# A streaming encoder step: frame tiles of the first group loaded two steps later, kept weight sums stored by the sync queue, and another order of the opening

## The chip, the cores and the metric

The kernel runs on one core of a Trainium2 chip. A core has five engines with queues of their own: TensorE (PE, matrix products; PEld is its weight load), VectorE (DVE), ScalarE (ACT), GpSimd (POOL) and SyncE (SP, which here only issues transfers). Each engine works through its instructions in the order in which they stand, and semaphores make one wait for another. The metric is the device time of one execution in microseconds, lower is better; the time given is the median of several runs.

## The reference

One step of a streaming encoder layer (depth 1): 2048 frames of a new stream and 32 of a running one, 1024 channels, all in float32.

```
hn   = rmsnorm(h, g_mix)
proj = hn @ w_in                       # 1024 x 3072: hA, bA, cA, zA, vB, zB of 512 columns each
yA   = bA * causal_conv3(cA * hA) * silu(zA)
yB   = (pooled(vB) - vB, per-group linear map, scale) * silu(zB)     # windows 2, 4, 8, 16
h    = h + concat(yA, yB) @ w_out
gate = sigmoid(rmsnorm(h, g_ple) @ w_ple_gate)
h    = h + (p @ w_ple) * gate
y    = rmsnorm(h, g_final)             # and the last rows of cA*hA and vB as new states
```

## The kernel before, in words

**Numbers.** Every float32 operand of a large product is split into a high part, rounded to a type that TensorE multiplies in one pass, and a low part, the rest. `split` does it: ScalarE casts the high part, VectorE subtracts it from the source (lines 77 and 78). A product is three products: high by high, high by low, low by high.

**Groups.** The 2080 frames are five blocks of 416 (`NB`), taken in groups `[0, 1]`, `[2, 3]`, `[4]`. In each group the input projection runs over four units j of 128 columns. The very first unit computes its two blocks plainly (`Unit.plain`), block by block. The other units of the first two groups take the two blocks as a 2 by 2 scheme with seven products in place of eight (`Unit.seven`, `Unit.pair`): the frames go in as seven combinations (11, 21, T2, T1, T3, 22, T4), the weights of two kinds side by side (zb with v, c with h, za with b) as seven others. Sums of carried and fresh results are made by ScalarE (`carry`, line 866) and VectorE (`out`, line 869).

**The opening.** The gain row g_mix is spread over 128 partitions by two small products (`gm`, line 375), and VectorE copies them to `g_bc`. The frame tiles of block 0 (three of 128 rows, one with 32 rows each of blocks 0 and 1) are loaded, squared and summed on ScalarE (line 88), their rstd is made on GpSimd (lines 69 and 73), VectorE scales them by rstd and gain (line 406), TensorE turns them (line 413), and they are split into `B0`. Then the weights zb, v and c of the first unit are split. `project` runs the first product by high parts first (line 586), all others by `half_product` (line 571). The generator `second_block` puts block 1 and the combinations in between.

**Next group's frames.** While the first group computes, `next_columns` prepares the seven combinations for the second group, column by column (3, 0, 1, 2). Each step of `Unit.seven` calls `aside`, which advances it at a fixed pace. For a column `frame_sums` squares and scales two frame tiles, turns them, and writes seven split results into tiles of the pool `xin` (`staged`), each of which `to_memory` stores to memory through GpSimd's queue (line 482). `xin` has five slots and holds both the frame tiles `xt` and the staged results. `load_ahead` loads the next column's two frame tiles on the sync queue; it is called at the sixth of the column's steps (i == 5), behind the result "22" and ahead of "T2", "T3" and "T4".

**Kept sums.** `pair_weights` adds and subtracts the two kinds' raw weights (lines 547 and 535). In the first group the two results of a pair are stored to memory (`kept`, lines 552 and 553) and read again in the second group. The stores go through GpSimd's queue, which also carries the rstd steps and the stores of the staged results. The sync queue carries the loads of raw weights (line 508, a ring of four tiles `raws`), the loads of frame tiles (line 392) and the stores of y (line 712).

**What orders the work.** A tile framework places the instructions of each engine by its own reckoning and inserts the semaphores; `keep_in_program_order` pins single instructions. A tile in a ring waits until the previous user of its slot is through.

Of the kernel before, what the change touches and what calls it, by code (L numbers as in the profile page):

```python
# [9 lines left out]
F32 = mybir.dt.float32  # L10
# [5 lines left out]
P = 128  # L16
# [18 lines left out]
def trunk(ctx, tc, x_p, x_s, c_conv, c_pool, p_p, p_s, g_mix, w_in, conv_w, conv_b, pool_w,  # L35
# [294 lines left out]
    with ExitStack() as s1:  # L330
# [195 lines left out]
        def pair_weights(gi, ka, kb, j, name, ring, s_ring):  # L526
# [17 lines left out]
            else:  # L544
# [5 lines left out]
                if gi == 0:  # L550
                    kept[ka, j] = k1, k3 = [tc.dram_tile([P, KH, P], F32, name=f"kept_{name}_{q}") for q in (1, 3)]
                    nc.gpsimd.dma_start(k1, s_t)
                    nc.gpsimd.dma_start(k3, s3)
            src = {"11": a11, "12": a12, "S2": a11, "S1": s_t, "S3": s3, "S4": a12, "22": a22}
# [18 lines left out]

        begun = []

        def project(ps, w, tb):
            x = hn[tb]
            if begun:
                for half in range(2):
                    half_product(ps, w[half], x[half], half == 0, half == 1)  # L580
                return

            begun.append(tb)
            steps = sorted(((k, a, b) for k in range(KC) for a, b in ((0, 0), (0, 1), (1, 0))), key=lambda t: t[1:])
            for i, (k, a, b) in enumerate(steps):
                nc.tensor.matmul(ps[:, :NB], w[k // KH][:, k % KH, a], x[k // KH][:, k % KH, b], start=i == 0,
                                 stop=i == len(steps) - 1)


        B0 = {}  # L590
        ahead0 = [x_tile(f"0_{c}", [x_rows(0, c)]) for c in range(3)]
        short0 = x_tile("0_3", [x_rows(0, 3), x_rows(1, 3)])
# [76 lines left out]
        class Unit:  # L669
# [98 lines left out]
            def plain(self):  # L768
                tbs, j, tag, zs, V, U, c_s = self.tbs, self.j, self.tag, self.zs, self.V, self.U, self.c_s
                blocks = range(len(tbs))  # L770

                def product_of(kind, b, w):
                    ps = bank(f"{kind}{tag}_{tbs[b]}")
                    project(ps, w, tbs[b])
                    return ps[:, :NB]
# [730 lines left out]
```

## Time and profile before

| what | us |
|---|---|
| median of three runs | 945.69 (944.71 to 946.76) |
| the profiled execution | 946.5, of which the span of the core's work is 944.7 |
| TensorE busy | 922.9 |
| VectorE busy | 717.3 |
| ScalarE busy | 481.3 |
| GpSimd busy | 137.0 |
| transfers | 190.05 MB, mean 201 GB/s |

Times in the profile are counted from the start of the span. A row of the time order reads: start, length, engine, line, operation, result<-inputs, shape, how many, and in brackets how long the engine had stood idle before it and what released it. A row of a stretch reads: length, then busy time of TensorE, its weight loads, VectorE, ScalarE and GpSimd, the granted clock of TensorE, the busy share of the transfer engines, and GB/s. A row of waits reads: who waited for whom, us in total, times, longest. A row of transfers ends with the KB of each and the us from issue to landing; q0 is GpSimd's queue, with packets, MB and its share of the transfer engines.

### The profile page before, as it was taken

To read this page: it belongs to the slowest core of one execution; us is meant where nothing else is said; L and a number is where in the kernel's file an instruction comes from. 1 tells how busy PE (TensorE), PEld (TensorE's weight loads), DVE (VectorE), ACT (ScalarE), POOL (GpSimd) and SP (SyncE) were. 2 spreads that over 40 slices of the span, in tenths; PEclk is the share of its full clock that TensorE was granted. 3 is DMA by queue.
4 is the path that set the end of the run, shared out by engine and by line. 5 is a ranking of instruction groups with operands and counts; after the bars stand their busy time and mean duration, and the time that the engine had idled before them with its cause. 6 is when DMAs were issued, how large, how long until landed. Compare 5 with 4: busy or idle time off the path is not lost.

```text
span 944.7 us, 13128 instructions
## 1 busy us (share of the span) xinstructions
PE 922.9 (98%) x4599; PEld 832.6 (88%) x4599; DVE 717.3 (76%) x1212; ACT 481.3 (51%) x890; POOL 137.0 (14%) x262
## 2 busy tenths in 40 slices
PE   7999999898999999999999999999999999999996
PEld 5999999898999999999999987888878868888885
DVE  6797998788676877776777588766554798888995
ACT  5554555463344554443554356434434885556564
POOL 2202333230100120000000011211111000211113
PEclk9999999999999999999999999999999999999999
DMA  8347686686972554618655349875785884566562
GB/s 252 95 125 199 190 262 215 198 247 182 417 253 90 180 185 131 208 57 291 177 175 174 129 145 315 270 199 159 222 255 160 309 277 127 198 232 222 207 206 111
DMA packets 132639, 190.05 MB, mean 201 GB/s; under 512 B 11740, under 2 KB 101084, under 8 KB 131293
## 3 DMA queue, kind: packets, MB, share of 16 engines
q1 hardware_dynamic: 115149, 134.06, 45.4%
q0 software_dynamic: 14688, 49.65, 16.0%
q10 hardware_dynamic: 2736, 5.51, 1.8%
q8 instruction: 36, 0.59, 0.3%
q14 instruction: 30, 0.25, 0.1%
HBM read 129.59 MB, written 59.58 MB: 200 GB/s over the span
## 4 chain that ended last, share of the span: by engine, by line
PE 77%; DVE 2%; ACT 1%; issue 0%; POOL 0%; POOLq 0%; ACTq 0%
PE x_o L167 9%; PE x_g L167 9%; PE x_zab L571 5%; PE e L102 5%; PE z_g L167 5%; PE x_ch L571 5%; PE x_zbv L571 5%; PE z_o L167 4%; PE z_ch L571 3%; PE z_zbv L571 2%; PE z_zab L571 2%; PE y_g L167 2%; PE y_o L167 2%; PE b L571 2%; PE za L571 2%; PE c L571 2%
## 5 line engine op out<-in xcount | busy, mean ns | idle before, releaser
L77 ACT CAST y_S<-y_fS 128x512 fp32r<-128x512 f32 x32 | 19.5, 621 | 43.9 <-PE x_o L167 19.4
L102 PE MATMUL e<-wq,pps 128*128 128x512 f32 (+1 forms) x156 | 38.9, 399 | 0.2 <-ACT pps L77 0.2
L571 PE MATMUL z_ch<-B,w_ch_S 128*128 128x416 f32 x168 | 35.9, 364 | 3.3 <-ACT U L866 3.3
L406 DVE SCALAR_TENSOR_TENSOR xt<-xt,rstd_x,g_bc 128x1024 f32<-128x1024 f32 (+2 forms) x18 | 23.1, 1282 | 19.1 <-POOL rstd_x L73 17.7
L571 PE MATMUL x_zab<-B,w_zab_S 128*128 128x416 f32 x168 | 34.6, 353 | 2.7 <-ACT V L866 2.0
L571 PEld LDWEIGHTS z_ch<-B,w_ch_S 128*128 128x128 f32 x168 | 32.4, 195 | 4.1 <-ACT U L866 3.6
L167 PE MATMUL x_g<-wg_b,g_S 128*128 128x512 f32 x128 | 35.9, 390 | 0.0
L167 PE MATMUL x_o<-wo_b,y_S 128*128 128x512 f32 x128 | 35.8, 391 | 0.0
L571 PEld LDWEIGHTS x_zab<-B,w_zab_S 128*128 128x128 f32 x168 | 31.1, 188 | 4.0 <-ACT V L866 2.6
L571 PE MATMUL z_zab<-B,w_zab_S 128*128 128x416 f32 x168 | 34.1, 351 | 0.5 <-ACT U L866 0.5
L571 PE MATMUL z_zbv<-B,w_zbv_S 128*128 128x416 f32 x168 | 34.2, 352 | 0.0
L571 PE MATMUL x_zbv<-B,w_zbv_S 128*128 128x416 f32 x168 | 34.1, 351 | 0.0
L571 PE MATMUL x_ch<-B,w_ch_S 128*128 128x416 f32 x168 | 34.0, 351 | 0.0
L102 PEld LDWEIGHTS e<-wq,pps 128*128 128x128 f32 (+1 forms) x156 | 27.4, 182 | 6.9 <-ACT pps L77 0.5
L571 PEld LDWEIGHTS z_zab<-B,w_zab_S 128*128 128x128 f32 x168 | 31.3, 188 | 1.1 <-ACT U L866 0.8
L69 POOL TENSOR_SCALAR ms_f<-ssq_f 128x1 f32<-128x1 f32 (+1 forms) x15 | 8.8, 588 | 160.7 <-ACT junk L88 160.7
L571 PEld LDWEIGHTS x_ch<-B,w_ch_S 128*128 128x128 f32 x168 | 31.4, 188 | 0.3
L571 PEld LDWEIGHTS x_zbv<-B,w_zbv_S 128*128 128x128 f32 x168 | 31.3, 188 | 0.3
L571 PEld LDWEIGHTS z_zbv<-B,w_zbv_S 128*128 128x128 f32 x168 | 31.2, 188 | 0.4
L77 ACT CAST y<-y 128x512 fp32r<-128x512 f32 x24 | 14.8, 618 | 28.7 <-PE x_o L167 14.0
L1328 DVE SCALAR_TENSOR_TENSOR h<-h,rstd_f,g_bc 128x1024 f32<-128x1024 f32 (+1 forms) x15 | 19.3, 1284 | 12.7 <-POOL rstd_f L73 12.7
L167 PEld LDWEIGHTS x_o<-wo_b,y_S 128*128 128x128 f32 x128 | 24.0, 188 | 5.1 <-ACT c_o L1132 0.3
(582 smaller groups left out, 2670.8 us busy)
## 6 DMA issues: line engine op xcount, KB each, us to landing
y<-y_d SPq DMA_DIRECT2D x16, 512.0 KB, 7.7
x<-in_x_prompt_dram SPq DMA_DIRECT2D x16, 512.0 KB, 6.7
h_d<-x SPq DMA_DIRECT2D x16, 512.0 KB, 3.4
h<-h_d SPq DMA_DIRECT2D x16, 512.0 KB, 5.1
xt<-in_x_prompt_dram SPq DMA_DIRECT2D x15, 512.0 KB, 12.0
e<-e_d SPq DMA_DIRECT2D x15, 512.0 KB, 5.1
out_dram<-h POOLq DMA_DIRECT2D x14, 512.0 KB, 3.0
p_dT<-T POOLq DMA_DIRECT2D x12, 512.0 KB, 5.3
```

What stands on the lines that cost most here:

```text
L69: nc.gpsimd.tensor_scalar(ms[:n], ssq[:n], scalar1=1.0 / D, scalar2=EPS, op0=ALU.mult, op1=ALU.add)
L77: ins = nc.scalar.copy(hi, src)
L102: nc.tensor.matmul(ps[:n], pps[:, a, k, :n], wp[k][b][:, cs], start=k + q == 0, stop=k == 1 and q == 2)
L167: nc.tensor.matmul(ps[:n], lhs[:, k, a, :n], w[b][:, k], start=start and k + q == 0, stop=k == KH - 1 and q == 2, skip_group_check=True)
L406: nc.vector.scalar_tensor_tensor(xt[:n], xt[:n], r[:n], g_bc[:n], op0=ALU.mult, op1=ALU.mult)
L571: nc.tensor.matmul(ps[:, :NB], lhs[:, k, x], b[:, k, y], start=start and k + q == 0, stop=stop and k == KH - 1 and q == 2, skip_group_chec ...
L1328: nc.vector.scalar_tensor_tensor(h[:n], h[:n], rf[:n], g_bc[:n], op0=ALU.mult, op1=ALU.mult)
```

## The change

Three things change.

1. In `next_columns` the next column's frame tiles are loaded at i == 7 instead of i == 5: behind the last but one of the results.
2. The 18 stores of kept sums (nine pairs of kinds in the first group) go through the sync queue instead of GpSimd's.
3. The opening is written out. The two products of g_mix stay in their banks: VectorE scales the first frame tiles from there, in halves, and ScalarE copies them to `g_bc` later. TensorE gets 14 transposes of the identity whose results are not used, into the bank that the short tile takes later: seven behind the products of g_mix, and two, three and two behind the first three tiles' transposes. Casts and subtractions of the first block are put in a fixed order, one cast goes to VectorE, and the first halves of the zb weight are cast ahead of the short tile's. The first 72 products no longer run zb, then v, then c, but high by high for zb, v and c, then high by low for the three, then low by high (`first_products`).

```diff
@@ the opening
+        pg = [tbank(f"gm_{half}") for half in range(2)]
         for half in range(2):
-            cs = slice(half * NH, half * NH + NH)
-            pg = tbank(f"gm_{half}")
-            nc.tensor.matmul(pg, ones, gm_row[:, cs], start=True, stop=True)
-            nc.vector.tensor_copy(g_bc[:, cs], pg)
+            nc.tensor.matmul(pg[half], ones, gm_row[:, half * NH:half * NH + NH], start=True, stop=True)
+
+        def fill(n, t):
+            for _ in range(n):
+                tc.keep_in_program_order(nc.tensor.transpose(t[:, :P], ident, ident))
+
+        short_bank = bank("pt0_3")
+        fill(7, short_bank)
@@ pair_weights
-                    nc.gpsimd.dma_start(k1, s_t)
-                    nc.gpsimd.dma_start(k3, s3)
+                    nc.sync.dma_start(k1, s_t)
+                    nc.sync.dma_start(k3, s3)
@@ the first products
-        begun = []
-
         def project(ps, w, tb):
             x = hn[tb]
-            if begun:
-                for half in range(2):
-                    half_product(ps, w[half], x[half], half == 0, half == 1)
-                return
-
-            begun.append(tb)
-            steps = sorted(((k, a, b) for k in range(KC) for a, b in ((0, 0), (0, 1), (1, 0))), key=lambda t: t[1:])
-            for i, (k, a, b) in enumerate(steps):
-                nc.tensor.matmul(ps[:, :NB], w[k // KH][:, k % KH, a], x[k // KH][:, k % KH, b], start=i == 0,
-                                 stop=i == len(steps) - 1)
+            for half in range(2):
+                half_product(ps, w[half], x[half], half == 0, half == 1)
+
+        def first_products(ws):
+            x = hn[0]
+            out = {kind: bank(f"{kind}0_0_0") for kind in ws}
+            for a, b in ((0, 0), (0, 1), (1, 0)):
+                for kind, w in ws.items():
+                    for k in range(KC):
+                        ins = nc.tensor.matmul(out[kind][:, :NB], w[k // KH][:, k % KH, a], x[k // KH][:, k % KH, b],
+                                               start=a + b + k == 0, stop=a == 1 and k == KC - 1, skip_group_check=True)
+                        if a + b + k or kind != "zb":
+                            in_turn(ins)
+            return out
@@ the first block
-        for c, x in enumerate([*ahead0, short0]):
-            normal(x)
-            n = P if c < 3 else DEC
-            for half, q in enumerate(("11", "21")):
-                put(B0[q][:, :, :, c * P:c * P + n], turn(x, half, f"pt0_{c}_{half}", bank)[:, :, :n])
+        def first_normal(x):
+            xt, m, r = x
+            for half in range(2):
+                h = xt[:m, half * NH:half * NH + NH]
+                in_turn(nc.vector.scalar_tensor_tensor(h, h, r[:m], pg[half][:m], op0=ALU.mult, op1=ALU.mult))
+        ...
+        for c in range(3):
+            first_x.append(x_stat(ahead0[c], True))
+        first_tile(0)
+        first_hi(0, 0)
+        first_x.append(x_stat(short0, True))
+        short0 = first_x[3]
+        first_tile(1)
+        first_hi(0, 1)
+        first_lo(0, 0)
+        for half in range(2):
+            first_hi(1, half)
+        first_tile(2)
+        first_hi(2, 0)
+        first_tile(3)
+        first_hi(2, 1, nc.vector.tensor_copy)
+        raw = raw_weight("zb", 0, "firstzb")
+        first_zb = [wtile(f"w_firstzb_{half}") for half in range(2)]
+        for half, t in enumerate(first_zb):
+            in_turn(nc.scalar.copy(t[:, :, 0], raw[:, half * KH:half * KH + KH]))
+        for half in range(2):
+            first_hi(3, half)
+        for c in range(4):
+            for half in range(2):
+                if c + half:
+                    first_lo(c, half)
         hn[0] = B0["11"], B0["21"]
-        first_w.extend([weights(kind, 0, f"first{kind}") for kind in ("zb", "v", "c")])
+        for half, t in enumerate(first_zb):
+            nc.vector.tensor_tensor(t[:, :, 1], raw[:, half * KH:half * KH + KH], t[:, :, 0].bitcast(F32), op=ALU.subtract)
+        first_w.extend([first_zb, *(weights(kind, 0, f"first{kind}") for kind in ("v", "c"))])
+        for half in range(2):
+            nc.scalar.copy(g_bc[:, half * NH:half * NH + NH], pg[half])
@@ Unit.plain
+                    first.update(first_products(dict(zb=wz, v=wv, c=wc)))
@@ next_columns
-                    if i == 5 and after is not None:
+                    if i == 7 and after is not None:
                         load_ahead(1, after)
```

`first_tile(c)` scales and turns tile c and adds the fills; `first_hi` and `first_lo` make the high and the low part of one half tile.

More of the change, by code (lines that the diff above doesn't have):

```diff
@@ L590, in trunk @@
         B0 = {}
-        ahead0 = [x_tile(f"0_{c}", [x_rows(0, c)]) for c in range(3)]
-        short0 = x_tile("0_3", [x_rows(0, 3), x_rows(1, 3)])
+        ahead0 = [x_load(f"0_{c}", [x_rows(0, c)]) for c in range(3)]
+        short0 = x_load("0_3", [x_rows(0, 3), x_rows(1, 3)])
         B0.update(six(0))
-        for c, x in enumerate([*ahead0, short0]):
-            normal(x)
-            n = P if c < 3 else DEC
-            for half, q in enumerate(("11", "21")):
-                put(B0[q][:, :, :, c * P:c * P + n], turn(x, half, f"pt0_{c}_{half}", bank)[:, :, :n])
@@ L599, in trunk, with in_turn, first_turn @@
-        hn[0] = B0["11"], B0["21"]
-        first_w.extend([weights(kind, 0, f"first{kind}") for kind in ("zb", "v", "c")])
+        def in_turn(ins):
+            tc.keep_in_program_order(ins)
+        def first_normal(x):
[3 more added lines that the diff above has]
+                in_turn(nc.vector.scalar_tensor_tensor(h, h, r[:m], pg[half][:m], op0=ALU.mult, op1=ALU.mult))
+        def first_turn(c, x):
+            xt, m, _ = x
+            if c < 3:
+                return [turn(x, half, f"pt0_{c}_{half}", bank) for half in range(2)]
+            t = short_bank
+            for k in range(KC):
+                tc.keep_in_program_order(nc.tensor.transpose(t[:, k * m:k * m + m], xt[:m, k * P:(k + 1) * P], ident[:m, :m]))
+            t = t.rearrange("p (k t) -> p k t", k=KC)
+            return t[:, :KH], t[:, KH:]
@@ new lines, in trunk, with place0, first_hi, first_lo @@
+        first_x, turned_x = [], {}
+        def place0(c, half):
+            n = P if c < 3 else DEC
+            piece = B0[("11", "21")[half]][:, :, :, c * P:c * P + n]
+            return piece[:, :, 0], piece[:, :, 1], turned_x[c][half][:, :, :n]
+        def first_hi(c, half, copy=nc.scalar.copy):
+            hi, _, src = place0(c, half)
+            in_turn(copy(hi, src))
+        def first_lo(c, half):
+            hi, lo, src = place0(c, half)
+            in_turn(nc.vector.tensor_tensor(lo, src, hi.bitcast(F32), op=ALU.subtract))
@@ L770, in plain @@
                 blocks = range(len(tbs))
+                first = {}
                 def product_of(kind, b, w):
+                    if b == 0 and kind in first:
+                        return first.pop(kind)[:, :NB]
                     ps = bank(f"{kind}{tag}_{tbs[b]}")
```

5 lines of the change are left out of this document (added).

## The prediction

> **What bounds the kernel now.** I read the page first, then busy time by stretch, then TensorE's waits, then the order of time around the stretches that have idle time.
>
> ```profile
> span 944.7 us, 13128 instructions
> PE 922.9 (98%) x4599; PEld 832.6 (88%) x4599; DVE 717.3 (76%) x1212; ACT 481.3 (51%) x890; POOL 137.0 (14%) x262
> ```
>
> TensorE is busy for 922.9 of 944.7 us, so at most 21.8 us of waiting is to be had, and only in the stretches where it lies. The stretches (TensorE's column is the first after the length) show them:
>
> ```profile
> 140.00:160.00 20.00, 20.00 (x114) 19.46 (x113) 18.03 (x29) 12.46 (x25) 4.83 (x8) 1.00 0.62 188
> 160.00:180.00 20.00, 17.31 (x89) 16.17 (x88) 15.18 (x27) 7.46 (x14) 5.29 (x7) 1.00 0.74 240
> 180.00:200.00 20.00, 18.58 (x104) 17.72 (x104) 18.80 (x32) 14.38 (x29) 7.79 (x12) 1.00 0.62 181
> 200.00:220.00 20.00, 17.66 (x94) 17.15 (x92) 15.36 (x27) 6.20 (x13) 3.36 (x6) 1.00 1.04 297
> 220.00:240.00 20.00, 19.08 (x93) 18.74 (x94) 19.17 (x33) 9.13 (x17) 2.16 (x4) 0.91 0.54 183
> ```
>
> From 160 to 240 us TensorE lacks 2.69 + 1.42 + 2.34 + 0.92 = 7.4 us, and in the last of these its granted clock is 0.91. Before that it is full. Its waits from 30 to 300 us name them:
>
> ```profile
> PE z_ch L571 <- ACT U L866: 3.3, 1, 3.3
> PE x_zab L571 <- ACT V L866: 2.0, 1, 2.0
> PE pt_g L413 <- DVE 11_1_2_1964 L78: 1.0, 1, 1.0
> PE x_zab L571 <- DVE w_zab_S L78: 0.7, 1, 0.7
> PE z_zab L571 <- ACT U L866: 0.5, 1, 0.5
> ```
>
> So the change can win in three places: the opening, the stop at 172 us (2.0 + 0.7), and the stop at 218 us (3.3).
>
> **The opening.** Time order of the first 42 us:
>
> ```profile
> 9.55 1.06 ACT L88 ACTIVATE junk<-xt 128x1024 bf16<-128x1024 f32 x1 [2.60 <-DMA xt<-in_x_prompt_dram]
> 16.44 3.14 PE L586 MATMUL zb<-B,w_firstzb 128*128 128x416 f32 x8
> 23.01 4.51 PE L571 MATMUL v<-B,w_firstv 128*128 128x416 f32 x23
> 27.36 1.04 PE L413 MATMUL pt<-ident,xt 128*128 128x128 f32 x8
> 28.15 4.78 PE L571 MATMUL c<-B,w_firstc 128*128 128x416 f32 x24
> 31.84 0.58 DVE L78 TENSOR_TENSOR pp<-pl,pp 128x416 fp32r<-128x416 f32 x1
> 32.34 1.28 DVE L78 TENSOR_TENSOR B<-pt,B 128x512 fp32r<-128x512 f32 x2
> 34.14 2.87 DVE L78 TENSOR_TENSOR B<-pt,B 128x512 fp32r<-128x512 f32 x6
> 37.19 4.51 PE L571 MATMUL zb<-B,w_firstzb 128*128 128x416 f32 x23
> ```
>
> The first eight products take 3.14 us, 0.39 each, where 23 later ones take 4.51, 0.196 each: they run at half speed. The change keeps TensorE at work before them (14 transposes of the identity, 7 + 2 + 3 + 2), and deals the first 72 products out so that the high parts of zb, v and c come first, while VectorE still makes the low parts. The first product itself hardly moves: the third frame tile lands at 9.55 us either way, and behind it ScalarE has still a square (1.06), casts of tiles and of the weight. I put it at 16.2. Then 72 products of 0.19 end at 16.2 + 13.7 = 29.9. Before, they ended at 28.15 + 4.78 = 32.9, with 8 transposes (1.0) between that now come behind; so TensorE is 2.0 us ahead. VectorE is less so: the second block's low parts wait for pp, and pp in the new order for the copy of c; from 29.9 that is three steps of 0.5 to 0.6, so pp's low part ends at about 31.6 (before, 32.4), and the eight low parts behind it (1.28 + 2.87 = 4.15 us) at 35.7, where they ended at 34.14 + 2.87 = 37.0. That is 1.3 us, and the dense run of zb at 37.19 hangs on it. Not seen in this trace: whether the fills bring full speed by 16 us. If not, 8 x 0.19 = 1.5 of it is lost and 0.5 is left; and the fills, 2 x 0.13 = 0.26 each at half speed (from the row at 27.36), could hold up a tile's transposes by two of them, 0.5. Bounds 0 to 2.0; I take **1.5 us**, near the VectorE row. The gain copies that leave VectorE (two) go to ScalarE behind the weight casts; the half-width scalings add four instructions for the same elements. Neither stands on the path worked out above.
>
> By the Trainium skill, "TensorE: Matmul & The Clock Gate", Part 1, the array starts at half clock and is released after about 3.4 us of sustained work; the slow first eight agree. Fourteen fills with gaps between might not count as sustained by that rule, and the opening's gain would then be its lower bound.
>
> **The stop at 172 us: frame tiles two steps later.** One column of frame tiles passes through a ring of five slots: two frame tiles, and staged results that go to memory through GpSimd's queue.
>
> ```profile
> 157.95 1.69 SPq L392 DMA_DIRECT2D xt<-in_x_prompt_dram x2
> 161.65 0.85 POOL L482 DMA_DIRECT2D p_d<-22_1_1_1730  x1 [0.35 <-DVE 22_1_1_1730 L78]
> 168.42 0.62 ACT L77 CAST T<-f_g 128x512 fp32r<-128x512 f32 x1 [7.19 <-DMA p_d<-21_1_1_1710]
> 169.95 0.62 ACT L77 CAST T<-f_g 128x512 fp32r<-128x512 f32 x1 [0.90 <-DMA p_d<-22_1_1_1730]
> 173.50 0.49 ACT L866 COPY V<-x_zab 128x416 f32<-128x416 f32 x1
> 174.03 0.65 PE L571 MATMUL x_zab<-B,w_zab_S 128*128 128x416 f32 x2 [2.01 <-ACT V L866]
> ```
>
> ScalarE stands 7.19 us at T3 until the store of 21 has landed, then at T4 until 22's has; behind them in its order stands the copy of V that TensorE wants. Loading the next pair two steps later leaves the two slots of the spent frame tiles to T2 and T3, so these two wait for nothing. T4 still takes 22's slot and waits for 22's store. What changes for that store is its company: one of the two frame tiles now needs the slot of 21's store and is issued only once this has landed. Two landings bound it:
>
> ```profile
> p_d<-22_1_0_1409 POOLq DMA_DIRECT2D x1, 512.0 KB, 4.3
> p_d<-22_1_1_1730 POOLq DMA_DIRECT2D x1, 512.0 KB, 8.2
> ```
>
> The same store took 4.3 us a column earlier. At 8.2 nothing is won; at 4.3 the whole 2.0 + 0.7 goes. One of two competing tiles is gone, and half a kept store; half of the 3.9 us between them is 2.0. I take **2.0 us** (bounds 0 to 2.7). T3's low part on VectorE also comes out of T4's way. The stops of 1.0 and 0.5 I leave, since they come from VectorE's and ScalarE's own order.
>
> **The stop at 218 us: kept sums on the sync queue.** Eighteen stores of 256 KB leave GpSimd's queue.
>
> ```profile
> 199.86 0.63 SPq L508 DMA_DIRECT2D raw_zab_3b<-in_w_in_dram  x1
> 202.56 0.55 POOL L553 DMA_DIRECT2D kept_ch<-raw_ch_3b  x1 [0.47 <-DVE raw_ch_3b L535]
> 214.78 0.69 DVE L547 TENSOR_TENSOR s_zab<-raw_zab_3b 128x512 f32<-128x512 f32 x1 [4.61 <-DMA raw_zab_3b<-in_w_in_dram]
> 212.97 2.43 PE L571 MATMUL z_ch<-B,w_ch_S 128*128 128x416 f32 x12
> 220.92 4.09 PE L571 MATMUL z_ch<-B,w_ch_S 128*128 128x416 f32 x12 [3.26 <-ACT U L866]
> 195.90:215.00 19.10, 19.10 (x103) 18.90 (x102) 14.46 (x26) 9.20 (x18) 5.37 (x7) 1.00 1.03 291
> q0 software_dynamic: 1019, 3.64, 67.6%
> ```
>
> VectorE stands 4.61 us until raw_zab_3b lands, 14.9 us after its issue; the pooling chain stands behind it in VectorE's order, ScalarE's cast and copy of U behind that, and TensorE 3.26 us at the end. The transfers are full from 196 to 215 us (share 1.03), and GpSimd's queue q0 takes 67.6% of the engines. In it are two stores of kept_ch, 0.52 MB, 0.52 / 291 GB/s = 1.8 us. In the changed order they stand behind raw_zab_3b in the sync queue, so they no longer take turns with it. Not all of that came ahead of the load: I take q0's share of it, 0.676 x 1.8 = 1.2 (bounds 0 to 1.8). Then the idle time is 2.1 us, about that of the stop at 172, in whose stretch (160 to 180) the granted clock stayed 1.00; after 3.26 idle twelve took 4.09 instead of 2.43. So 1.66 more goes: **2.9 us** (bounds 0 to 3.26 + 1.66 = 4.9).
>
> On the sync queue each kept store stands ahead of loads and waits for its sum. Its sums are ready, by the stores' issue times on GpSimd, before the load behind them could start; raw_ch_0a alone is held, until the sum that GpSimd stored at 202.56, and is not read until the next group. Of the loads behind the later frame tiles raw_zab_2a moves most, behind two stores of y:
>
> ```profile
> 135.83 0.81 SPq L712 DMA_DIRECT2D y_d<-c_s  x2
> 153.60 1.22 ACT L77 CAST w_zab<-raw_zab_2a 128x512 fp32r<-128x512 f32 x2
> ```
>
> It is cast 17 us later. So nothing is charged; if that cover were gone, TensorE would wait for what is missing. GpSimd loses 18 issues of about 0.6 us; no chain above goes through them.
>
> **Sum**: 1.5 + 2.0 + 2.9 = 6.4 us. The profiled execution is 944.7 us of span within 946.5 us, 0.8 above the median of the runs, 945.69. Taken off the median: **939.3 us**.
>
> **The rivals.**
> *The load gains nothing.* What holds raw_zab_3b are the 3.64 MB of q0, of which kept_ch is a seventh; moved to the other queue, the bytes are the same. Then the stop at 218 stays whole and the time is 945.69 - 1.5 - 2.0 = 942.2. Against it: the two kept stores no longer go in turns with the load but behind it. By the Trainium skill ("Trainium Kernel Development and Optimization", Key Constraints) all queues run on the same 16 engines and spreading issues over them saves only issue time, which is this rival. "DMA: Bandwidth & Descriptors", Queues, rings and completion order, has each engine go round between queue rows, which favours a load whose rival is put behind it in its own row.
>
> *The waits stay.* T4 waits for 22 as long as now, and the stop at 218 stays: only the opening is won, 944.2, within what a measurement of this kernel tells from no change (0.2%, 1.9 us).
>
> *Slower: the frame tiles come too late.* The second tile of the next pair is issued only when 21's store has landed.
>
> ```profile
> DMA to landing us min/median/max: 6.2/7.8/17.8
> 181.12 1.05 ACT L88 ACTIVATE junk<-xt 128x1024 bf16<-128x1024 f32 x1
> ```
>
> That store's landing at 168.4, less the 1.5 us of the opening, less some company, gives an issue at 165.4; the second square is due at 181.1 - 3.5 = 177.6. A landing within 12.2 us costs nothing; the median is 7.8, the longest 17.8. At 17.8 ScalarE stands 5.6 us at the square, with the copies that free TensorE's banks behind it, and the stop at 218 is as before or worse by a cold start (1.66): 945.69 - 3.5 + 5.6 + 1.66 = 949.5. It ends slower from a landing of 12.2 + 3.5 = 15.7 us.
>
> **How the numbers follow.** All three gains, in some part: 0.48, with 936 to 942 as its own range. The load gains nothing: 0.15 (942.2). All three at their upper bounds, 2.0 + 2.7 + 4.9 = 9.6: 0.07 (936.1). Only the opening, or gains and losses that cancel: 0.13. Late frame tiles: 0.17. So faster 0.70, same 0.13, slower 0.17. The range goes from 935.5, just under the upper bounds, to 946.5, which takes in the case of no change and leaves out most of the slower one.
>
> **What would show it.** Right: the first eight zb products at 0.2 us each, and the dense run of zb in the second block near 35.7; T3's cast without a wait and T4's before 168 less the opening's gain; no wait of x_zab over 0.7; s_zab less than 13.5 us behind the issue of raw_zab_3b; z_ch's twelve in 2.4. Wrong: first products still at 0.39; ScalarE idle at a square for a frame tile; a new wait of TensorE between 37 and 160 us, where the list of waits has none; or s_zab as late as before.

## The result and the profile after

The changed kernel takes 939.48 us (median of six runs, 938.53 to 941.28) beside 945.9 for the kernel before (six runs, 944.71 to 946.84): a ratio of 0.9937, interval 0.9926 to 0.9949, that is 6.0 us (4.8 to 7.0) saved. The forecast was 939.3. A second measurement, with the experiments below, gave 0.9945 (0.9928 to 0.9963), 5.2 us.

The head of the page of the changed kernel, then its busy time by stretch (columns as before: TensorE first, then its weight loads, VectorE, ScalarE, GpSimd, granted clock, share of the transfer engines, GB/s):

```profile
span 937.3 us, 13159 instructions
PE 921.0 (98%) x4613; PEld 830.4 (89%) x4613; DVE 716.3 (76%) x1215; ACT 481.4 (51%) x891; POOL 128.2 (14%) x244
```

```profile
160.00:180.00 20.00, 18.52 (x94) 17.05 (x93) 15.95 (x26) 9.18 (x17) 5.08 (x8) 1.00 0.81 257
180.00:200.00 20.00, 19.03 (x108) 18.51 (x108) 19.76 (x36) 10.76 (x21) 6.25 (x8) 1.00 0.67 184
200.00:220.00 20.00, 18.72 (x98) 17.87 (x97) 17.34 (x29) 8.67 (x16) 0.00 (x0) 1.00 0.91 270
220.00:240.00 20.00, 20.00 (x108) 19.80 (x107) 19.57 (x35) 9.28 (x17) 3.78 (x7) 1.00 0.82 307
```

From 160 to 240 us TensorE now lacks 1.48 + 0.97 + 1.28 = 3.7 us, where it lacked 7.4, and the clock of 0.91 in the last stretch is gone. Its waits from 30 to 300 us:

```profile
PE z_ch L577 <- ACT U L947: 1.3, 1, 1.3
PE pt_g L419 <- DVE 11_1_2_1981 L78: 1.0, 1, 1.0
PE x_zab L577 <- DVE w_zab_S L78: 0.7, 1, 0.7
PE z_zab L577 <- ACT U L947: 0.5, 1, 0.5
PE x_zab L577 <- ACT V L947: 0.3, 1, 0.3
```

The wait for V has gone from 2.0 to 0.3, that for U from 3.3 to 1.3; the other three stand as they did. Now the three places in the order of time. The opening (the third frame tile's square, the first products, the second block's low parts, the dense run of zb):

```profile
8.27 1.06 ACT L88 ACTIVATE junk<-xt 128x1024 bf16<-128x1024 f32 x1 [0.71 <-DMA xt<-in_x_prompt_dram]
14.65 1.73 PE L592 MATMUL zb<-B,w_firstzb 128*128 128x416 f32 x8 [0.83 <-DVE B L637]
30.68 4.07 DVE L78 TENSOR_TENSOR B<-pt,B 128x512 fp32r<-128x512 f32 x8
34.89 4.51 PE L577 MATMUL zb<-B,w_firstzb 128*128 128x416 f32 x23
```

The first eight run at 0.22 us each, and the dense run starts at 34.89 instead of 37.19, 2.3 us earlier and, as forecast, right behind the eight low parts (30.68 + 4.07 = 34.75). But the third frame tile is squared 1.3 us earlier than before, which nothing in the change explains. The stop at 172 us:

```profile
158.25 7.22 SPq L398 DMA_DIRECT2D xt<-in_x_prompt_dram  x2
159.04 0.63 ACT L77 CAST T<-f_g 128x512 fp32r<-128x512 f32 x1
159.57 0.85 POOL L488 DMA_DIRECT2D p_d<-22_1_1_1747  x1 [0.35 <-DVE 22_1_1_1747 L78]
166.65 0.62 ACT L77 CAST T<-f_g 128x512 fp32r<-128x512 f32 x1 [6.97 <-DMA p_d<-22_1_1_1747]
170.26 0.64 PE L577 MATMUL x_zab<-B,w_zab_S 128*128 128x416 f32 x2 [0.32 <-ACT V L947]
177.36 1.05 ACT L88 ACTIVATE junk<-xt 128x1024 bf16<-128x1024 f32 x1
```

T3's cast (159.04) waits for nothing. T4's starts 7.1 us behind the issue of 22's store (8.3 before). The second frame tile is issued only when the first row's 7.22 us are over, at 165.5, and its square at 177.36 waits for nothing. The stop at 218 us:

```profile
196.10 0.63 SPq L514 DMA_DIRECT2D raw_zab_3b<-in_w_in_dram  x1
197.32 7.18 SPq L558 DMA_DIRECT2D kept_ch<-s_ch  x1
209.04 0.69 DVE L553 TENSOR_TENSOR s_zab<-raw_zab_3b 128x512 f32<-128x512 f32 x1 [2.63 <-DMA kept_ch<-s_ch]
215.18 2.53 PE L577 MATMUL z_ch<-B,w_ch_S 128*128 128x416 f32 x12 [1.28 <-ACT U L947]
```

s_zab starts 12.9 us behind the load's issue instead of 14.9, and the twelve products behind the stop take 2.53 instead of 4.09. What releases s_zab is no longer the load but the store of kept_ch: s_zab overwrites the buffer that this store reads (`s` has one buffer).

### The profile page after: what moved, and what is told of

Same layout as the page of the kernel before. It is cut to its first block, busy times and chain, and to the rows that moved or that the text cites. A ratio compares the mean times of both kernels' runs of the same rounds, so it can differ in the third digit from the quotient of the medians.

```text
span 937.3 us, 13159 instructions
## 1 busy us (share of the span) xinstructions
PE 921.0 (98%) x4613; PEld 830.4 (89%) x4613; DVE 716.3 (76%) x1215; ACT 481.4 (51%) x891; POOL 128.2 (14%) x244
## 4 chain that ended last, share of the span: by engine, by line
PE 75%; DVE 2%; ACT 1%; DMA 1%; issue 1%; POOL 0%; POOLq 0%; DVEq 0%; ACTq 0%
PE x_o L167 9%; PE x_g L167 9%; PE x_zab L577 5%; PE e L102 5%; PE z_g L167 5%; PE z_o L167 4%; PE x_ch L577 4%; PE x_zbv L577 4%; PE z_zab L577 2%; PE y_g L167 2%; PE z_ch L577 2%; PE y_o L167 2%; PE b L577 2%; PE v L577 2%; PE z_zbv L577 2%; PE c L577 2%
## 5 line engine op out<-in xcount | busy, mean ns | idle before, releaser
L412 DVE SCALAR_TENSOR_TENSOR xt<-xt,rstd_x,g_bc 128x1024 f32<-128x1024 f32 (+2 forms) x14 | 18.0, 1283 | 15.6 <-POOL rstd_x L73 14.4
L77 ACT CAST y<-y 128x512 fp32r<-128x512 f32 x24 | 14.9, 620 | 28.8 <-PE x_o L167 13.8
```

The costliest lines, as they stand in the source:

```text
L77: ins = nc.scalar.copy(hi, src)
L412: nc.vector.scalar_tensor_tensor(xt[:n], xt[:n], r[:n], g_bc[:n], op0=ALU.mult, op1=ALU.mult)
```

## The experiments

In each, the us won or lost are the ratio's distance from 1 times 946, with the interval. Only the code lines that matter are shown; a minus line is of the kernel that was edited, the one before or the changed one. A single profile's rows differ by up to 1 or 2 us from execution to execution, so places are compared over all profiles that share the part in question; the table behind the experiments has them.

**1. The new beginning alone** on the kernel before: frame tiles loaded at i == 5 and kept stores on GpSimd's queue, as they were (shown as an edit of the changed kernel).

```diff
-                    if i == 7 and after is not None:
+                    if i == 5 and after is not None:
-                    nc.sync.dma_start(k1, s_t)
-                    nc.sync.dma_start(k3, s3)
+                    nc.gpsimd.dma_start(k1, s_t)
+                    nc.gpsimd.dma_start(k3, s3)
```

> The kernel before with the new beginning alone. The reading of the changed kernel (ahead of the stop at 172 us its x_zab runs at 164.12, before at 166.20) gives the beginning 2.1 us: then the time is 2.1 under that of the kernel before, about 943.7, the first zb products start near 14.7, and the stops at 172 and 218 us stay (x_zab waits 2.0, z_ch 3.3). The prediction's own term gives 1.5 less, 944.3, with the first product at 16.2. Rival: part of the 2.1 us is the third frame tile, which landed earlier in that one execution by chance; then its square starts near 9.5 again and the gain is 1 us or less.

Measured: 945.32 beside 946.13, ratio 0.9995 (0.9979 to 1.001): 0.5 us won (from 2.0 won to 0.9 lost). The time order of it:

```profile
9.44 1.06 ACT L88 ACTIVATE junk<-xt 128x1024 bf16<-128x1024 f32 x1 [2.44 <-DMA xt<-in_x_prompt_dram]
15.78 1.75 PE L592 MATMUL zb<-B,w_firstzb 128*128 128x416 f32 x8 [0.83 <-DVE B L637]
36.02 4.51 PE L577 MATMUL zb<-B,w_firstzb 128*128 128x416 f32 x23
173.53 0.65 PE L577 MATMUL x_zab<-B,w_zab_S 128*128 128x416 f32 x2 [2.64 <-ACT V L947]
174.86 3.45 PE L577 MATMUL x_zab<-B,w_zab_S 128*128 128x416 f32 x10 [0.68 <-DVE w_zab_S L78]
```

The third tile lands near 9.5 again, and the dense run starts at 36.02, close to the forecast of 35.7. So 1.1 of the 2.3 us in the changed kernel's first profile was one early landing: the rival's reading, as to the profile (experiment 7 bears it out). In this execution 0.6 of the lead went at the stop at 172 us (2.64 instead of 2.01), where ten products then also ran slower (3.45 instead of 2.15). The timing alone doesn't tell 0.5 from 1.5.

**2. The frame tiles later, alone.**

```diff
-                    if i == 5 and after is not None:
+                    if i == 7 and after is not None:
```

> The kernel before with the frame tiles two steps later alone. By the prediction's mechanism T3's cast waits for nothing, 22's store lands in 6 to 7.5 us and x_zab's wait of 2.0 falls to 0.3: 1.7 us under the kernel before, about 944.0, with the stop of z_ch at 218 us as before (3.3 and twelve products in 4.1 us). Rival 1: the store's landing became shorter through the other parts of the change; then x_zab still waits over 1.2 and less than 0.8 us is won. Rival 2: the frame tiles' place also empties the transfers ahead of 218 us; then the stop there shrinks too and 4 us or more are won, 941.7 or less.

Measured: 944.03, ratio 0.9983 (0.9969 to 0.9998): 1.6 us won (0.2 to 2.9).

```profile
170.49 0.62 ACT L77 CAST T<-f_g 128x512 fp32r<-128x512 f32 x1 [7.13 <-DMA p_d<-22_1_1_1730]
174.10 0.65 PE L571 MATMUL x_zab<-B,w_zab_S 128*128 128x416 f32 x2 [0.47 <-ACT V L866]
220.29 3.96 PE L571 MATMUL z_ch<-B,w_ch_S 128*128 128x416 f32 x12 [2.55 <-ACT U L866]
```

The wait for V is 0.47, the stop at 218 us stays: the mechanism of the prediction, and neither rival.

**3. The kept stores on the sync queue, alone.**

```diff
-                    nc.gpsimd.dma_start(k1, s_t)
-                    nc.gpsimd.dma_start(k3, s3)
+                    nc.sync.dma_start(k1, s_t)
+                    nc.sync.dma_start(k3, s3)
```

> The kernel before with the kept sums stored by the sync queue alone. By the prediction's mechanism s_zab starts less than 13.5 us behind the issue of raw_zab_3b, z_ch waits 1.3 to 2.1 us and its twelve products take 2.5: 2.9 to 3.6 us under the kernel before, 942.1 to 942.8; x_zab's wait at 172 us stays at 2.0. Rival 1 (the load gains nothing): the bytes are the same, z_ch still waits 3 us or more, same time as before, 945.7. Rival 2: the gain at 218 us comes only together with the later frame tiles, which put other transfers into that stretch; then less than 1 us is won here.

Measured: 943.38, ratio 0.9976 (0.9963 to 0.9988): 2.3 us won (1.1 to 3.5), where 2.9 to 3.6 were expected.

```profile
201.76 0.64 SPq L508 DMA_DIRECT2D raw_zab_3b<-in_w_in_dram  x1
214.55 0.69 DVE L547 TENSOR_TENSOR s_zab<-raw_zab_3b 128x512 f32<-128x512 f32 x1 [2.47 <-DMA kept_ch<-s_ch]
220.69 2.53 PE L571 MATMUL z_ch<-B,w_ch_S 128*128 128x416 f32 x12 [1.13 <-ACT U L866]
```

s_zab is 12.8 us behind the issue, z_ch waits 1.13. The load gains, against the rival that it can't; and here too s_zab ends up waiting for the store.

**4. Two of the eighteen stores.** Which ones matter: only kept_ch of the last unit, the two behind the load.

```diff
-                    nc.gpsimd.dma_start(k1, s_t)
-                    nc.gpsimd.dma_start(k3, s3)
+                    (nc.sync if (ka, j) == ("c", 3) else nc.gpsimd).dma_start(k1, s_t)
+                    (nc.sync if (ka, j) == ("c", 3) else nc.gpsimd).dma_start(k3, s3)
```

> The kernel before with two of the eighteen kept stores alone on the sync queue: those of kept_ch in the last unit, which were issued just behind the load raw_zab_3b. Theory (these two took turns with the load): s_zab starts 12.6 to 13.1 us behind the load's issue and z_ch waits 1.1 to 1.5, as with all eighteen moved; 2 to 3 us under the kernel before. Rival: the load gains from the other sixteen, which leave GpSimd's queue earlier in the kernel; then s_zab starts 14 us or more behind the issue, z_ch waits 2.4 or more, and less than 0.8 us is won.

Measured: 943.92 beside 946.54, ratio 0.9973 (0.9962 to 0.9984): 2.6 us won (1.5 to 3.6), as much as all eighteen.

```profile
174.78 1.06 PE L571 MATMUL x_zab<-B,w_zab_S 128*128 128x416 f32 x2 [2.26 <-ACT V L866]
176.11 3.83 PE L571 MATMUL x_zab<-B,w_zab_S 128*128 128x416 f32 x10 [0.27 <-DVE w_zab_S L78]
...
213.67 0.69 DVE L547 TENSOR_TENSOR s_zab<-raw_zab_3b 128x512 f32<-128x512 f32 x1 [2.67 <-DMA kept_ch<-s_ch]
```

s_zab is 13.0 us behind the issue (200.68). So no gain of the sixteen others shows, in the row or in the time. The first two rows show a stop of 2.26 us behind which products run at half speed; more on that below.

**5. The changed kernel without the fourteen transposes of the identity.**

```diff
-        fill(7, short_bank)
-            if c < 3:
-                fill((2, 3, 2)[c], short_bank)
```

> The changed kernel without the fourteen transposes of the identity. If they bring TensorE to full speed, the first eight zb products take 0.39 us each again instead of 0.22, some of the tiles' transposes too, and the time is 1.4 to 2 us over that of the changed kernel, about 941.2. Rival: the 32 transposes of the frame tiles, or the mere time since the first product, bring full speed by themselves; then the eight take 0.22 and the time is that of the changed kernel, 939.5.

Measured: 943.32, ratio 0.9972 (0.9959 to 0.9985): 2.6 us under the kernel before, so 2.6 to 3.4 over the changed one, where 1.4 to 2 were expected.

```profile
12.51 1.31 PE L418 MATMUL pt<-ident,xt 128*128 128x128 f32 x8 [1.49 <-DVE xt L610]
15.79 3.11 PE L591 MATMUL zb<-B,w_firstzb 128*128 128x416 f32 x8 [0.83 <-DVE B L636]
38.27 3.94 PE L576 MATMUL zb<-B,w_firstzb 128*128 128x416 f32 x20
175.53 0.64 PE L576 MATMUL x_zab<-B,w_zab_S 128*128 128x416 f32 x2 [1.67 <-ACT V L944]
```

The first eight are back at 0.39 us each and the dense run starts at 38.27, no earlier than with the old beginning. The third frame tile came as in experiment 1 (its square at 9.45 and 9.44) and the first product too (15.79 and 15.78), so in the opening these two profiles differ by the fills alone, and the dense run by 2.25 us. Casts in order and dealt-out products alone win nothing here: as far as one profile shows, the fills are the whole of the opening's gain. In this pair they kept full speed rather than reached it: the third tile's transposes took 1.31 us without them, as with them (1.38 in experiment 1), where the kernel before took 1.97. After the stops of 1.49 and 0.83 us the first eight products, and the eight behind them (2.98 us), ran at half speed. The rest of the loss in this profile is a slower landing of 22's store (8.4 us), which made x_zab wait 1.67.

**6. The changed kernel without the new beginning** (experiments 2 and 3 together, shown as an edit of the kernel before).

```diff
-                    if i == 5 and after is not None:
+                    if i == 7 and after is not None:
-                    nc.gpsimd.dma_start(k1, s_t)
-                    nc.gpsimd.dma_start(k3, s3)
+                    nc.sync.dma_start(k1, s_t)
+                    nc.sync.dma_start(k3, s3)
```

> The changed kernel with the old beginning: frame tiles later and kept stores on the sync queue, nothing else. Seven traces with the new beginning start the dense zb run of the second block at 36.0 us on the mean, four with the old one at 37.8. If that lead of 1.8 us is kept to the end, this kernel stands 1.8 us over the changed one, whose two measurements are 6.0 and 5.2 us under the kernel before: so 3.4 to 4.2 us under the kernel before, near 942. Rival: the lead is lost at the stops, since those end by transfers (the beginning alone won 0.5 to 0.8 us); then it is within 0.8 us of the changed kernel, 4.4 us or more under the kernel before.

Measured: 942.6 beside 946.38, ratio 0.9953 (0.9934 to 0.9971): 4.4 us won (2.7 to 6.2), or 3.8 by the medians. By the ratios that leaves 0.8 to 1.6 us for the opening, between the two readings, and doesn't settle them. Its profile had an early dense run for the old beginning:

```profile
36.68 4.51 PE L571 MATMUL zb<-B,w_firstzb 128*128 128x416 f32 x23
```

**7. The changed kernel once more.**

> The changed kernel once more, beside the three that follow. In its first profile the third frame tile was squared at 8.27 us, in the five other executions seen at 9.44 to 9.85. If that was one early landing, this profile has it near 9.5 again, the first zb product near 15.8 and the dense zb run of the second block at 36.0 instead of 34.9: the opening then gains what the new beginning alone showed, 1.2 to 2.2 us, and the span is about 1.1 us longer than the first, 938.4. Rival: the order of the loads makes it early; then 8.3 and 34.9 again.

Measured: 941.01 beside 945.79, ratio 0.9945 (0.9928 to 0.9963).

```profile
9.85 1.06 ACT L88 ACTIVATE junk<-xt 128x1024 bf16<-128x1024 f32 x1 [2.65 <-DMA xt<-in_x_prompt_dram]
16.37 2.75 PE L592 MATMUL zb<-B,w_firstzb 128*128 128x416 f32 x8 [0.83 <-DVE B L637]
37.66 4.50 PE L577 MATMUL zb<-B,w_firstzb 128*128 128x416 f32 x23
```

The early landing of the first profile was one execution's. Here the tile came at 9.85, TensorE stood 1.7 us for it, and the first eight fell to 0.34 us each (clock 0.60 from 16 to 20 us) in spite of the fills: in this one execution they didn't keep full speed over a wait of this size.

**8. s_zab in a buffer of its own** (the changed kernel; a tile of the ring of frame sums, with its place in VectorE's order held behind the second window sum, from which two more follow; the list `win_step` holds those sums).

```diff
-                    steps = [self.pair(*pairs[i + n], ring[i + n], ftile if n else None) for n in range(side_by_side)]
+                    steps = [self.pair(*pairs[i + n], ring[i + n], ftile if n or (self.gi, j, i) == (0, 3, 2) else None) for n in range(side_by_side)]
-                nc.vector.tensor_tensor(s_t, a21, a22, op=ALU.add)
+                with tc.issue_after(win_step[-3].ins) if s_ring and gi == 0 else ExitStack(): nc.vector.tensor_tensor(s_t, a21, a22, op=ALU.add)
```

> The changed kernel with s_zab of the last unit in a buffer of its own, not the one that the store of s_ch is still reading. Theory: since the stores moved behind the load, s_zab waits for the store kept_ch<-s_ch, not for raw_zab_3b; then s_zab starts 1 to 2.6 us earlier than 12.9 us behind the load's issue, z_ch's wait of 1.3 falls to under 0.3, and the time is 1.0 to 1.6 us under that of the changed kernel. Rival: load and store land together, because they share the same transfers in the same queue; then s_zab starts 12.5 to 12.9 us behind the issue, now released by raw_zab_3b, and the time is the same within 0.4 us.

Measured: 941.57, ratio 0.9955 (0.994 to 0.9971), no faster than the changed kernel.

```profile
209.74 0.69 DVE L553 TENSOR_TENSOR s_zab<-raw_zab_3b 128x512 f32<-128x512 f32 x1 [2.02 <-DMA raw_zab_3b<-in_w_in_dram]
215.88 2.54 PE L577 MATMUL z_ch<-B,w_ch_S 128*128 128x416 f32 x12 [0.69 <-ACT U L947]
219.39 2.53 PE L577 MATMUL x_ch<-B_T,w_ch 128*128 128x416 f32 x12 [0.97 <-DVE U L950]
```

s_zab now starts 12.3 us behind the issue (197.40), released by the load: the store had held it 0.6 us, less than the theory's 1 to 2.6. z_ch's wait halves. But a wait of 0.97 takes the gain's place: with the old buffer free earlier, the planner drew the next group's sum s_zbv ahead of U's sum in VectorE's order. There VectorE stands 0.90 us until the load raw_zbv_0b has landed, and x_ch waits for U behind it.

**9. The frame tiles one step later still**, behind T4 (the changed kernel; the first column has one step less).

```diff
-                    if i == 7 and after is not None:
+                    if i == (7 if c == 3 else 8) and after is not None:
```

> The changed kernel with the frame tiles loaded one step later still, behind T4. Then T4 takes the slot of T1's store, issued 6 us ahead of 22's. Theory (the slot's store is what T4 waits for): T4's cast has no wait of 7 us, x_zab's wait of 0.3 to 1.7 us for V is gone, and 0.3 to 1.0 us is won; the second tile of the next pair now waits for 22's store and lands near 176 to 178 us in this kernel's time, its square is due at 177.4. Rival: that tile comes late, ScalarE stands at its square for 1 us or more with the copies of z_zab behind it, and the kernel is 0.5 to 2 us slower than the changed one.

Measured: 937.45, ratio 0.991 (0.9893 to 0.9927): 8.5 us won (6.9 to 10.1), 3.3 more than the changed kernel beside it, where 0.3 to 1.0 were expected.

```profile
159.92 1.15 ACT L77 CAST T<-f_g 128x512 fp32r<-128x512 f32 x2
170.65 2.43 PE L577 MATMUL x_zab<-B,w_zab_S 128*128 128x416 f32 x12
176.42 1.06 ACT L88 ACTIVATE junk<-xt 128x1024 bf16<-128x1024 f32 x1 [1.24 <-DMA xt<-in_x_prompt_dram]
```

And from the list of TensorE's waits of the same kernel:

```profile
PE pt_g L419 <- DVE 11_1_2_1981 L78: 0.2, 1, 0.2
```

T3 and T4 are cast together without a wait, and x_zab runs without one, neither for V nor for w_zab_S: 0.45 + 0.70 less than in experiment 7's profile. The wait of pt_g falls from 1.0 to 0.2 as well. That is some 2 us; the rest of the 3.3 is within the two intervals. The late frame tile makes ScalarE stand 1.24 us at its square, as the rival had it, but TensorE doesn't notice.

**10. Both of the last two edits.**

> Both of the last two edits on the changed kernel. If each gains and they do not meet (the one acts at 166 to 172 us, the other at 206 to 216 us), the gains add: 1.3 to 2.5 us under the changed kernel, about 937.5. If the late frame tile costs as the rival of the one edit has it, the sum is 0 to 1 us.

Measured: 939.83, ratio 0.9934 (0.9914 to 0.9954): worse than the frame tiles alone, and not the 937.5 of two gains that add.

```profile
215.66 0.69 DVE L553 TENSOR_TENSOR s_zbv<-raw_zbv_0b 128x512 f32<-128x512 f32 x1 [2.28 <-DMA raw_zbv_0b<-in_w_in_dram]
```

VectorE stands 2.28 us for that load, U's sum stands behind it, and x_ch waits 2.36 us for U. The two edits do meet, through VectorE's order.

**11. The same, with VectorE's order held**: the next group's s_zbv is kept behind the last unit's convolution, where it stood (the list `conv_step` holds its steps). Every engine's order is then that of experiment 9, and only s_zab's buffer differs. The new line alone is shown.

```diff
+                with tc.issue_after((win_step[-3] if gi == 0 else conv_step[-1]).ins) if (s_ring and gi == 0) or (gi == 1 and j == 0 and ka == 'zb') else ExitStack(): nc.vector.tensor_tensor(s_t, a21, a22, op=ALU.add)
```

> The frame tiles behind T4, s_zab in a buffer of its own, and VectorE's order held as it is without that buffer (s_zbv of the next group was drawn ahead of U's sum and made x_ch wait 1.0 to 2.4 us). Theory: s_zab starts at the load's landing, 12.3 to 12.4 us behind its issue, z_ch waits 0.7 instead of 1.5, x_ch 0.3: 0.8 us under the kernel with the frame tiles behind T4 alone, which stood 8.3 us under the kernel before; so about 9.1 under it. Rival: TensorE's next wait takes the 0.8 back (x_ch for U's sum, w_zab_S); then the same time within 0.3 us.

Measured: 936.85 beside 946.54, ratio 0.9898 (0.9879 to 0.9917): 9.6 us won (7.9 to 11.4), the fastest kernel of the study.

```profile
206.34 0.69 DVE L553 TENSOR_TENSOR s_zab<-raw_zab_3b 128x512 f32<-128x512 f32 x1 [2.11 <-DMA raw_zab_3b<-in_w_in_dram]
212.48 2.53 PE L577 MATMUL z_ch<-B,w_ch_S 128*128 128x416 f32 x12 [0.77 <-ACT U L947]
215.00 2.54 PE L577 MATMUL x_ch<-B_T,w_ch 128*128 128x416 f32 x12
```

z_ch waits 0.77 and x_ch nothing that its row shows, as the theory says. Its 1.1 us beside experiment 9 is inside the two intervals, so the 0.7 of the profile is shown by the rows, not by the time.

**12. More fills** (experiment 9 with seven transposes of the identity behind the second tile instead of three).

```diff
-                fill((2, 3, 2)[c], short_bank)
+                fill((2, 7, 2)[c], short_bank)
```

> The frame tiles behind T4, and seven transposes of the identity instead of three behind the second tile's, where TensorE waits 0.4 to 1.7 us for the third frame tile. Theory: in executions in which that tile lands late (a wait of 1.7 us, after which the first eight zb products took 2.75 us instead of 1.75) the added 0.5 us of work keeps full speed, and nothing is lost where it lands early: same median or up to 0.5 us under the kernel with the frame tiles behind T4, first eight at 1.75. Rival: the added transposes hold up the third tile's by up to 0.5 us and the opening ends that much later: 0.1 to 0.5 us over it.

Measured: 937.96, ratio 0.9912 (0.9896 to 0.9929), the same as experiment 9. The profile had an early third tile (8.96) and the eight at 1.75; the case in which the fills would help didn't come up, so the theory is neither shown nor refuted.

**The places over all profiles** (us; "behind issue" is s_zab's start less the issue of raw_zab_3b):

| place | old part | new part | mean gain |
|---|---|---|---|
| dense zb run of block 2 starts | 37.19, 38.24, 38.04, 37.56, 36.68 | 34.89, 36.02, 37.66, 35.90, 35.73, 35.83, 35.92 | 37.54 - 35.99 = 1.55 |
| x_zab waits for V at 172 (i == 5 or 7) | 2.01, 2.64, 2.24, 2.26 | 0.32, 0.47, 1.67, 0.45, 0.20, 0.46 | 2.29 - 0.60 = 1.69 |
| z_ch waits for U at 218 (stores by GpSimd or sync) | 3.26, 2.46, 2.55 | 1.28, 1.13, 1.13, 1.41, 1.40, 1.40 | 2.76 - 1.29 = 1.47 |
| the twelve products behind it | 4.09, 2.54, 3.96 | 2.53 each | 3.53 - 2.53 = 1.0 |
| s_zab behind issue | 14.9, 14.1, 14.2 | 12.8 to 13.1; own buffer 12.3, 12.4, 12.4 | |

Left out are experiments 5 and 12 in the first row, since they have other fills, experiments 9 to 12 in the rows of x_zab and z_ch, since their frame tiles come later still, and experiment 8 in those of z_ch, since s_zab has its own buffer there. With the old buffer, experiments 9 and 12 had z_ch waits of 1.50 and 1.30.

Two things hide in the table. The third frame tile's square was itself 0.4 us earlier on the mean in the new profiles (9.24 against 9.62); counted from it, the dense run starts 27.9 us behind in the old and 26.8 in the new, so 1.2 of the 1.55 is left. Whether the new order brings the tile earlier stays open. And in experiments 1 and 4 ten products behind x_zab's wait ran 1.30 and 1.68 us slower than at full speed; behind them TensorE's waits for pt_g and z_zab were together 0.9 and 1.5 us shorter than in the kernel before, so little of that is lost in the end.

The sum is 1.55 + 1.69 + 1.47 + 1.0 = 5.7 us, and the two timings of the changed kernel say 6.0 and 5.2. The single parts give 0.5 + 1.6 + 2.3 = 4.4 by their own timings, each within about 1.3 us, which doesn't contradict the others.

## Why the prediction was right

**The sum.** 1.5 + 2.0 + 2.9 = 6.4 was forecast; the places give 1.55, 1.69 and 2.5. Each term is of the right place and mechanism; the last two were a little large. That 939.48 lies 0.2 us from the forecast is luck: the same kernel gave 941.01 in experiment 7.

**The opening.** Right in size: 1.55 against 1.5 (1.2 from the tile's landing), with first products at 15.5 to 15.8 in five of the seven profiles (16.2 forecast) and the dense run at 35.7 to 36.0 (35.7). The step "the third frame tile lands at 9.55 us either way" held within 0.4 us in all profiles of this beginning but experiment 12's (8.96) and the first one of the changed kernel (8.27), and in this last the early landing made the gain look like 2.3. The step that failed is the lower bound: "if not, 8 x 0.19 = 1.5 of it is lost and 0.5 is left". Without the fills nothing is left (38.27 against 37.54), since not eight but sixteen products ran at half speed (3.11 + 2.98 us, with the fills 1.75 + 1.67). The Trainium skill's "TensorE: Matmul & The Clock Gate", Part 1, lets the array go to full clock after about 3.4 us of sustained work. The doubt that fills with gaps might not count was half right: with gaps of up to 1.1 us they counted in six of seven profiles, with a gap of 1.7 us (experiment 7) they did not.

**The stop at 172 us.** The landing of 22's store was put at half of the way from 8.2 to 4.3 us, that is 6.2; measured, T4's cast starts 7.0 to 7.2 us behind the issue in five profiles of six (8.4 in one), so the company of the one frame tile gone was worth 1.2, not 2.0. The side remark that T3's low part also comes out of T4's way is worth the rest: from T4's cast to V's copy it is 3.07 us now (166.65 to 169.72), 3.55 before, and 1.22 + 0.48 = 1.7, the whole of what the wait lost. One sign wasn't met: T4's cast came at 166.65, not before 168 less the opening's gain (166.5, or 165.7 by the 2.3 of that profile). That the waits of 1.0 (pt_g) and 0.5 (z_zab) stay was right for the change made, but the reason given, VectorE's and ScalarE's own order, was not the whole of it: with T4's wait gone too, pt_g's is 0.2 to 0.3 in the four profiles of experiments 9 to 12, and z_zab's is off the list in three of them (0.4 in experiment 9, where the frame tile came late). Most of both was the late T4 handed on.

**The stop at 218 us.** The two kept stores behind the load were named as what takes turns with it, and experiment 4 shows that these two are all of it. Their price was low: the load itself lands 2.0 us earlier, above the bound of 1.8 that their bytes gave (14.4 us behind its issue on the mean of the three old profiles, 12.4 in the three where s_zab has a buffer of its own and so shows the landing). What the prediction didn't see is the new wait: moved behind the load and held 7.2 us at the first one's issue, the stores come late, and s_zab, which overwrites the one buffer that they read, waits for the first of them. That gives back 0.6 us, so that the net 1.47 is near the 1.2 taken. "So nothing is charged" for the order of the sync queue was therefore wrong by this 0.6; for the loads behind it was right in the changed kernel (raw_ch_0a, issued at 205.27, is first read at 225.97), though the cover is thin: with another order on VectorE, raw_zbv_0b was waited for (experiments 8 and 10). The 1.66 for the slow twelve is their size in one execution; over three it is 1.0, since one of them ran at full speed after 2.46 us.

**The rivals.** "The load gains nothing" fell with experiments 3 and 4. For the Trainium skill that means: of the two rules named, "DMA: Bandwidth & Descriptors", Queues, rings and completion order (an engine goes round between queue rows) agrees with the trace, since two stores moved into the load's own row let it land 2.0 us earlier; "Trainium Kernel Development and Optimization", Key Constraints, by which spreading issues over engines saves only issue time, would have kept it at 14.4. But the first store was also held some 7 us at its issue, and the second stood behind it; whether it was the turns or that hold that kept them out of the load's way, no run here tells. "The waits stay" fell with experiments 2 and 3. "The frame tiles come too late" didn't happen. Its price, a standing of ScalarE charged in full, is in doubt too: in experiment 9 the square does wait 1.24 us, and that kernel is faster. A wait of the 5.6 us that the rival had wasn't seen.

## What to carry to other kernels

When a wait ends with a transfer, look at what else that transfer's buffer ring and queue make wait: the cure here was to choose which slot a result takes. T4 behind an old store instead of a fresh one gave the largest gain measured for a single edit, 3.3 us (experiment 9). Moving two stores behind a load helped the load here, but the store's source buffer stays taken that much longer; giving its next user a buffer of its own shortened TensorE's waits only where the other instructions' order was held while doing so (experiment 11 beside 8 and 10). One profile is one execution: a landing that is 1.3 us early or late looks like an effect of the change until a second profile is taken.

## What the runs showed of the hardware

**Half speed after a stop isn't a matter of its length alone.** After waits of 3.26, 2.55, 2.64 and 2.26 us the following products ran slow (twelve in 4.09, twelve in 3.96, ten in 3.45, ten in 3.83, where full speed is 2.4 to 2.5 for twelve); after 2.46, 2.36, 2.24 and 2.01 they didn't. In experiment 1 the two products right behind the wait of 2.64 us still ran at full speed (0.65), and the slow ten came behind a second stop of 0.68. Behind a long dense run, then, 2.0 us was free of this cost in these traces, 2.55 and more was not, and between them either happened; in the opening, where TensorE has been busy for a few us only, stops of 1.7 and 0.8 us were enough (experiment 7). The Trainium skill's "TensorE: Matmul & The Clock Gate", Part 1, has the array fall back after an idle window of about 3.4 us that runs freely; the mixture fits a free-running window, the losses at 2.3 us and the like don't fit its length.

**The clock column doesn't always show the slow beginning.** The stretch from 16 to 20 us in the profile of the kernel before, and in that of experiment 2:

```profile
16.00:20.00 4.00, 4.00 (x15) 3.73 (x14) 4.00 (x9) 3.75 (x9) 0.00 (x0) 1.00 0.83 286
```

```profile
16.00:20.00 4.00, 4.00 (x17) 3.75 (x16) 4.00 (x9) 3.43 (x8) 0.00 (x0) 0.50 0.79 290
```

The granted clock (third number from the end) is 1.00 in the one and 0.50 in the other, while the first eight products took 3.14 us in both. In the opening the durations of the products are the better witness.

**An issue can take 7 us on the sync queue.** The store kept_ch<-s_ch, whose data were ready, took 6.99 to 7.26 us to issue behind two loads of 512 KB in all eleven profiles in which it stands there (7.18 in the row shown above). It is the place and not the store: in the three profiles in which the stores are on GpSimd's queue, the load raw_ch_0a stands third behind the same two loads, and its issue took 7.21 to 7.24 us. What it waits for there, the profiles don't show.
